# A fourth buffer for the projections' split weights, and other places for the pools of the up projection, in a decoder layer

## The chip, the cores and the metric

The kernel runs on one core of a Trainium2 chip. Its time is the device time of one execution in microseconds (us). The core has a matrix engine (PE in the profile), a vector engine (DVE), a scalar engine (ACT), GpSimd (POOL), and a sync engine (SP) from whose queue most DMAs are issued; each engine takes its instructions in the order in which they stand in its own list.

## What is computed

One layer of a hybrid decoder on a sequence of 1024 tokens of width 1024, in float32. Three branches (an mLSTM, a differential attention, a cross-attention into a memory) each give 1024 features per token; each is projected, weighted by a gate, and summed; one more projection and a residual follow, and then an MLP with a squared ReLU:

```python
merged = g_m * (y_m @ w_proj_m[l]) + g_d * (y_d @ w_proj_d[l]) + g_c * (y_c @ w_proj_c[l])
x = x + merged @ w_out[l]
h2 = rms_norm(x, norm_mlp_g[l])
x = x + jnp.square(jax.nn.relu(h2 @ w_up[l])) @ w_down[l]
```

The widths are 1024 to 1024 for the four projections, 1024 to 4096 for `w_up` and 4096 to 1024 for `w_down`. What stands ahead of these lines (norm, input projection, the three branches, the gates) isn't touched by the change.

## The kernel before

Features lie on the partitions and tokens along the free axis. Every float32 operand of a matmul is split into two parts of a shorter format, hi = cast(x) on ACT and lo = x - hi on DVE (`split`, lines L111 and L112, and `split2`, L104 and L67, whose DVE half keeps its place in the program's order). A product is then three matmuls (`mm3`, L91): hi with hi, weight hi with lo of the other operand, weight lo with hi. So PE's second matmul on an operand can't start before DVE has made its lo half.

The change lies in `tail()`, which has two stages and is followed by a third, `down()`.

**Projections.** The loop over the branches b = 2, 0, 1 loads the branch's output as eight tiles `kt` (`k_tiles`, L1382, raw tiles `kraw`), splits them into the nine places ys0 to ys8, and goes through four groups g of 256 output features. A group's weights come as two halves: `load_w` loads a raw tile of 128x1024 (L137, pool `rp2`, two buffers) and splits it into a `w` tile of twice the size (pool `wp2`, three buffers). A fourth pass over g does the output projection with `wout`: for each of the four quarters of a group, `res` adds the residual (L1475, tile `gl`), stores the new x (L1476, `x1_d`, in the profile x_d), squares it (L1481), adds the square to `ssq` on POOL (L1482), and stores x times the norm's gain (L1484, L1485, h2, in the profile h_d).

**Up projection.** `wino` runs a product of 2x2 blocks with seven products instead of eight (`PROD`), over 16 groups u of 256 output features, four steps kp each. A step needs the operand `xo` of kp (four of them, kept through the stage: loaded as `xr` from h2, combined into `xts` by `wino_t`, L1241 to L1244, and split) and a weight tile `wo`: a raw tile `wraw` (L1273, four places in turn, wr0 to wr3) on which POOL does four operations (`wino_s`, L1259 to L1262), split into one of four places in turn (wop1, wop20, wop21, wop22). 21 matmuls of 128x512 make a step; each of the seven sums has its own bank of PSUM. After a group DVE combines the banks into u2, c11, u3, c21 (pool `ev`), multiplies them by the norm's factor `rb` (L1516), ACT applies ReLU and Square into `rq` (L1517, L1518) and stores it to `r_d` (L1519); a generator resumed later makes `xts` of it and stores that too (L1522). The norm's factor is made in `rstd` from `ssq` in the midst of the first groups: 16 matmuls `px`, a copy `st` (L1532), a power on POOL.

**Down projection.** `down()` opens its own pools over the places of the up projection. Its operands `xd` are the rows of `r_d`, loaded by `xdma` (L1611) and split by `xsplit`; its weights `wo` have three places (dwo0 to dwo2) and its raw tiles three (dwr0 to dwr2). The operand of the first step, q = 0, is in three tiles: dx00 (products' operands 0 to 2), dx01 (3, 4) and dx02 (5, 6); those of q = 1, 2, 3 are in two tiles each. It goes in 16 passes of four steps, again 21 matmuls a step.

All pools of SBUF are stacked in the order in which they are opened, and a pool that is opened over the place of a closed one waits, tile by tile, until what lay there has been read for the last time. The order of the instructions on each engine is made by a scheduler when the program is built, except where PE's (`pinned`), DVE's (`self.V`) and the split's order are kept.

Of the kernel before, what the change touches and what calls it, by code (L numbers as in the profile page):

```python
# [10 lines left out]
F32 = mybir.dt.float32  # L11
# [6 lines left out]
P = 128  # L18
# [53 lines left out]
class Layer:  # L72
# [1338 lines left out]
    def tail(self):  # L1411
# [5 lines left out]
        def fetch(d, f, hf):  # L1417
            t = self.gl.tile([P, 512], F32, tag="gl", name=self.name("gl"))
            nc.sync.dma_start(t, half(d, f, hf))
            return t  # L1420

        c9 = ExitStack()
        with ExitStack() as c0:
            E = lambda *x, **k: c0.enter_context(tc.tile_pool(*x, **k))
# [8 lines left out]
            with ExitStack() as c1:  # L1433
                E = lambda *x, **k: c1.enter_context(tc.tile_pool(*x, **k))
                self.pmm, self.kmm, self.nmm = Banks(E, "pmm2"), 8, 3
                if True:

                    mtp = E(name="mtp", bufs=1)
                    mlp = E(name="mlp", bufs=16)
                    op = E(name="op", bufs=2)  # L1440
                    hole = E(name="hole", bufs=1).tile([P, 7 * 256], F32, name="hole")
                    V.memset(hole[:, 0:1], 0.0)
                    ysp = Ring([E(name=f"ys{i}", bufs=1) for i in range(9)][::-1])
                    rawp = E(name="yrp", bufs=2)
                    self.rp = E(name="rp2", bufs=2)
                    self.wp = E(name="wp2", bufs=3)
                    hi = [[mtp.tile([P, 512], F32R, name=f"mh{k}_{hf}") for hf in range(2)] for k in range(NK)]
                    mg, lo = {}, {}
                    for bi, b in enumerate((2, 0, 1)):
                        ys = self.k_tiles(ysp, rawp, self.yd[b])  # L1450
                        for g in range(4):

                            def merge(m, hf, ps):
                                ft = g * 2 + m
                                t = fetch(self.gdr, b * 8 + ft, hf)
                                if bi == 0:
                                    mg[ft, hf] = mlp.tile([P, 512], F32, tag="ml", name=self.name("mg"))
                                o = mg[ft, hf] if bi == 0 else t
                                V.scalar_tensor_tensor(out=o, in0=t, scalar=1.0, in1=ps, op0=ALU.add, op1=ALU.mult)
                                if bi == 1:  # L1460
                                    G.tensor_add(mg[ft, hf], mg[ft, hf], t)
                                if bi == 2:
                                    V.tensor_add(t, mg[ft, hf], t)
                                    lo[ft, hf] = mlp.tile([P, 512], F32R, tag="ml", name=self.name("ml"))
                                    self.split(hi[ft][hf], lo[ft, hf], t)

                            w = self.load_w(a[("wpm", "wpd", "wpc")[b]][g], 256, 4)
                            self.group(w, lambda k, i, hf: cut(ys[k], i, hf), merge, g == 0)
                    for g in range(4):

                        def res(m, hf, ps):
                            f = g * 2 + m
                            s = slice(hf * 512, (hf + 1) * 512)
                            x = fetch(a["xT"], f, hf)
                            V.scalar_tensor_tensor(out=x, in0=ps, scalar=0.5, in1=x, op0=ALU.mult, op1=ALU.add)  # L1475
                            nc.sync.dma_start(half(self.x1d, f, hf), x)  # L1476
                            if f == 0:
                                nc.scalar.activation(ssq[:, s], x, AF.Square)
                            else:
                                q = op.tile([P, 512], F32, tag="sq", name=self.name("sq"))  # L1480
                                nc.scalar.activation(q, x, AF.Square)  # L1481
                                G.tensor_add(ssq[:, s], ssq[:, s], q)  # L1482
                            h = op.tile([P, 512], F32, tag="h2", name=self.name("h2"))
                            nc.scalar.activation(h, x, AF.Copy, scale=self.vec[:, R_MLP + f : R_MLP + f + 1])  # L1484
                            nc.sync.dma_start(half(self.h2d, f, hf), h)  # L1485

                        w = self.load_w(a["wout"][g], 256, 4)
                        self.group(w, lambda k, i, hf: lo[k, hf] if i else hi[k][hf], res, g == 0)

            self.pw = Banks(lambda *x, **k: c9.enter_context(tc.tile_pool(*x, **k)), "pw")  # L1490
            with ExitStack() as c1:
                E = lambda *x, **k: c1.enter_context(tc.tile_pool(*x, **k))
                one_ = lambda n: E(name=n, bufs=1)
                xo2, xo3, wr2, wr3, self.ev, wop1, self.xtp, self.xrp, xo0, xo1, wr0, wr1 = (
                    one_(n)
                    for n in ("xo2", "xo3", "wr2", "wr3", "ev", "wop1", "xtp", "xrp", "xo0", "xo1", "wr0", "wr1")
                )
                wop2 = [one_(f"wop2{i}") for i in range(3)]
                self.xop = (xo0, xo1, xo2, xo3)
                self.wrp, self.wop = Ring([wr0, wr1, wr2, wr3]), Ring([wop1, *wop2])  # L1500
                dp, ap = one_("dgp"), one_("prt")

                def load(kp):
                    b = self.xrp.tile([P, 4, 512], F32, tag="xr", name=self.name("xr"))
                    nc.sync.dma_start(
                        b.rearrange("p (k h) n -> p k (h n)", k=2),
                        self.h2d[2 * kp : 2 * kp + 2].rearrange("k p n -> p k n"),
                    )
                    return b

                def use_up(u, cs):

                    b = self.xrp.tile([P, 4, 512], F32, tag="xr", name=self.name("rq"))
                    for i in (1, 3, 2, 0):
                        hf = i % 2
                        self.V.tensor_mul(cs[i], cs[i], rb[:, hf * 512 : (hf + 1) * 512])  # L1516
                        self.A.activation(cs[i], cs[i], AF.Relu)  # L1517
                        self.A.activation(b[:, i], cs[i], AF.Square)  # L1518
                    self.A.dma_start(self.rd[u, :, 0:3], b[:, 1:4])  # L1519
                    yield  # L1520
                    t = self.wino_t(b, self.V)
                    nc.sync.dma_start(self.rd[u, :, 3:7], t)  # L1522
                    yield

                def rstd():

                    bank = yield
                    ps = self.pw.tile([P, 512], F32, tag=bank, name=self.name("px"))
                    for t in range(NT):
                        self.mm(ps[:, t : t + 1], ssq[:, t * P : (t + 1) * P], ones[:, 0:1], start=True, stop=True)  # L1530
                    st = dp.tile([P, NT], F32, tag="st", name="st2")
                    V.tensor_copy(st, ps[:, 0:NT])  # L1532
                    self.rsqrt_mean(st, st, D, NT)
                    bank = yield
                    dg = dp.tile([P, NT, P], F32, tag="dg", name="dg")
                    for t in range(NT):
                        V.tensor_scalar_mul(dg[:, t], self.ident, st[:, t : t + 1])
                    for hf in range(2):
                        bank = yield
                        ps = self.pw.tile([P, 512], F32, tag=bank, name=self.name("px"))  # L1540
                        for i in range(4):
                            self.mm(ps[:, i * P : (i + 1) * P], ones, dg[:, hf * 4 + i], start=True, stop=True)
                        nc.scalar.copy(rb[:, hf * 512 : (hf + 1) * 512], ps)
                    yield

                rs = rstd()
                next(rs)

                def parts():
                    t = [ap.tile([P, 512], F32, name=f"pt{i}") for i in range(3)]  # L1550
                    t += [self.gl.tile([P, 512], F32, tag="gl", name=f"pt{i}") for i in (3, 4)]
                    q = sp.tile([P, D], F32, tag="ssq", name="pt5")
                    return t + [q[:, 0:512], q[:, 512:]]

                self.wino([a["wup"][u] for u in range(16)], load, use_up, rs.send, parts)
# [340 lines left out]
```

## Time and profile before

| | |
|---|---|
| median of 3 runs | 2207.19 us (2204.16 to 2207.41) |
| the profiled execution | 2206.06 us, span of its records 2204.3 us |
| mean granted clock of PE | 0.994 of full speed |
| PE busy | 2156.7 us, 98% of the span |
| DVE, ACT, POOL busy | 1422.7, 1001.4, 566.6 us |
| moved by DMA | 281.46 MB, 128 GB/s on the mean |

The profile of one execution is read by views. The chain of waits follows the work back from the last instruction. The view of waits lists by engine and line what an engine sat idle for. The view of groups gives count, busy time and mean duration (ns) of instructions of one line, operation and shape. The view of windows gives, for each stretch, the busy time of each engine with the number of its instructions, and at the end PE's granted clock (1.00 is full speed), the share of DMA engines busy and the GB/s moved. The timeline lists instructions by start and length, merged where they are alike, with the idle time before them in brackets. The projections' part that the change touches begins at about 1190 us, the up projection at 1566 us, the down projection at 1885 us.

### The profile page before, as it was taken

To read this page: it belongs to the slowest core of one execution; us is meant where nothing else is said; L and a number is where in the kernel's file an instruction comes from. 1 tells how busy PE (TensorE), PEld (TensorE's weight loads), DVE (VectorE), ACT (ScalarE), POOL (GpSimd) and SP (SyncE) were. 2 spreads that over 40 slices of the span, in tenths; PEclk is the share of its full clock that TensorE was granted. 3 is DMA by queue.
4 is the path that set the end of the run, shared out by engine and by line. 5 is a ranking of instruction groups with operands and counts; after the bars stand their busy time and mean duration, and the time that the engine had idled before them with its cause. 6 is when DMAs were issued, how large, how long until landed. Compare 5 with 4: busy or idle time off the path is not lost.

```text
span 2204.3 us, 30709 instructions
## 1 busy us (share of the span) xinstructions
PE 2156.7 (98%) x11049; PEld 1856.0 (84%) x11049; DVE 1422.7 (65%) x2678; ACT 1001.4 (45%) x1998; POOL 566.6 (26%) x732
## 2 busy tenths in 40 slices
PE   7999999999999999999999999999999999999999
PEld 5877888898799999999878888887787888788887
DVE  6643565575447877777665432544688877867779
ACT  6543354454246666666554220224444444543332
POOL 2100000000211111111031003202657655565553
PEclk9999999999999999999999999999999999999999
DMA  6113222121443333333254543436435444854444
GB/s 244 36 68 116 62 91 68 44 82 48 150 126 92 89 88 93 94 82 82 84 170 131 204 149 119 139 110 210 151 111 197 158 149 147 322 195 156 143 142 166
DMA packets 137358, 281.46 MB, mean 128 GB/s; under 512 B 13137, under 2 KB 29814, under 8 KB 135158
## 3 DMA queue, kind: packets, MB, share of 16 engines
q1 hardware_dynamic: 130870, 259.58, 37.5%
q10 hardware_dynamic: 6336, 19.93, 2.3%
q8 instruction: 87, 1.43, 0.3%
q14 instruction: 65, 0.53, 0.1%
HBM read 182.95 MB, written 71.34 MB: 115 GB/s over the span
## 4 chain that ended last, share of the span: by engine, by line
PE 80%; DVE 7%; DMA 7%; ACT 2%; POOL 2%; issue 2%; SPq 0%; DVEq 0%; ACTq 0%; POOLq 0%
PE mm L91 47%; PE p L91 20%; PE sc L91 6%; PE po L91 3%; PE tp L94 3%; DVE acc L67 1%; DVE wo L67 1%; DMA wraw<-in_wdown 1%; PE pr L94 1%; DMA xd<-r_d 1%; DMA xr<-h_d 1%; DVE w L112 1%; DMA gl<-in_xT 1%; DMA x_d<-gl 1%; DMA raw<-in_wd 0%
## 5 line engine op out<-in xcount | busy, mean ns | idle before, releaser
L91 PE MATMUL mm<-w,hT 128*128 128x384 f32 (+3 forms) x2496 | 475.5, 333 | 6.9 <-ACT w L111 5.9
L91 PE MATMUL mm<-hT,w 128*128 128x512 f32 x1680 | 411.8, 396 | 0.0
L91 PEld LDWEIGHTS mm<-w,hT 128*128 128x128 f32 x2496 | 391.8, 190 | 19.3 <-ACT w L111 7.2
L91 PEld LDWEIGHTS mm<-hT,w 128*128 128x128 f32 x1680 | 308.5, 188 | 64.7
L91 PE MATMUL p<-xo,wo 128*128 128x512 f32 x1344 | 309.9, 392 | 6.3 <-DVE st L1532 3.2
L91 PE MATMUL p<-xd,wo 128*128 128x512 f32 x1344 | 310.0, 393 | 4.4 <-DVE c L67 1.8
L91 PEld LDWEIGHTS p<-xo,wo 128*128 128x128 f32 x1344 | 252.2, 189 | 62.7 <-DVE u L67 3.7
L91 PEld LDWEIGHTS p<-xd,wo 128*128 128x128 f32 x1344 | 254.0, 190 | 60.2 <-DVE c L67 2.9
L91 PE MATMUL mm<-kt,w 128*128 128x512 f32 x1152 | 262.3, 389 | 0.8 <-DVE kt L112 0.8
L91 PEld LDWEIGHTS mm<-kt,w 128*128 128x128 f32 x1152 | 215.9, 188 | 47.1 <-DVE kt L112 1.4
L111 ACT CAST w<-raw 128x256 fp32r<-128x256 f32 (+3 forms) x272 | 142.3, 545 | 155.5 <-PE mm L91 124.5
L112 DVE TENSOR_TENSOR w<-raw,w 128x256 fp32r<-128x256 f32 (+3 forms) x272 | 161.1, 613 | 76.7 <-ACT w L111 76.0
L104 ACT CAST wo<-wraw 128x896 fp32r<-128x896 f32 x122 | 114.9, 944 | 206.8 <-PE p L91 109.7
L67 DVE TENSOR_TENSOR wo<-wraw,wo 128x896 fp32r<-128x896 f32 x122 | 144.5, 1201 | 60.1 <-ACT wo L104 60.0
L1259 POOL TENSOR_TENSOR wraw<-wraw 128x128 f32<-128x128 f32 x128 | 95.9, 749 | 245.2 <-DMA wraw<-in_wdown 106.8
L1007 ACT ACTIVATE dpe<-sc,dst,drr 128x256 f32<-128x256 f32 (+7 forms) x128 | 106.6, 833 | 96.6 <-DVE dst L1003 91.8
L127 POOL TENSOR_SCALAR hss<-hss 128x4 f32<-128x4 f32 x8 | 3.3, 409 | 415.2 <-ACT mscr L752 272.9
L999 DVE CUSTOM_DVE_ANT_0 sc<-sc,tmask 128x256 f32<-128x256 f32 (+7 forms) x128 | 97.2, 759 | 14.0 <-PE sc L91 13.4
L91 PE MATMUL sc<-dk,dq 128*128 128x512 f32 (+3 forms) x384 | 92.2, 348 | 0.0
L1262 POOL TENSOR_TENSOR wraw<-wraw 128x128 f32<-128x128 f32 x128 | 88.2, 689 | 9.9
L1261 POOL TENSOR_TENSOR wraw<-wraw 128x128 f32<-128x128 f32 x128 | 88.7, 693 | 0.0
L104 ACT CAST xd<-xd 128x1536 fp32r<-128x1536 f32 (+2 forms) x36 | 54.9, 1528 | 72.0 <-DMA xd<-r_d 72.0
(308 smaller groups left out, 3093.3 us busy)
## 6 DMA issues: line engine op xcount, KB each, us to landing
dk<-dsg SPq DMA_DIRECT2D x64, 256.0 KB, 4.3
wraw<-in_wup SPq DMA_DIRECT2D x64, 256.0 KB, 3.3
r_d<-xts SPq DMA_DIRECT2D x16, 1024.0 KB, 4.1
wraw<-in_wdown SPq DMA_DIRECT2D x64, 256.0 KB, 3.1
xd<-r_d SPq DMA_DIRECT2D x19, 768.0 KB, 7.6
xd<-r_d SPq DMA_DIRECT2D x14, 1024.0 KB, 7.2
raw<-in_wd SPq DMA_DIRECT2D x32, 384.0 KB, 3.3
kraw<-y SPq DMA_DIRECT2D x24, 512.0 KB, 4.2
```

The source lines that it names most:

```text
L67: return self.tc.keep_in_program_order(f(*a, **k))
L91: self.pin(self.nc.tensor.matmul(out, l, r, start=start, stop=stop))
L94: self.pin(self.nc.tensor.transpose(out, x, self.ident))
L104: self.A.copy(hi, src)
L111: nc.scalar.copy(hi, src)
L112: nc.vector.tensor_sub(lo, src, f32(hi))
L127: g.tensor_scalar(r, ss, 1.0 / width, EPS, op0=ALU.mult, op1=ALU.add)
L999: V.tensor_tensor_reduce(out=sc[:, 0:n], in0=sc[:, 0:n], in1=self.tmask[:, D - n : D], scale=1.0, scalar=-3.0e38, op0=ALU.add, op1=ALU.max ...
L1007: nc.scalar.activation(pe[c][:, 0:n], sc[:, 0:n], AF.Exp, bias=t8[:, 2 + c : 3 + c], scale=rr[:, i, c : c + 1], accum_out=t8[:, 4 + c : 5 ...
L1259: G.tensor_add(r[:, 4], r[:, 0], r[:, 3])
L1261: G.tensor_sub(r[:, 6], r[:, 1], r[:, 0])
L1262: G.tensor_sub(r[:, 7], r[:, 2], r[:, 5])
```

## The change

The diff has two edits in `tail()`; `down()` isn't edited.

```diff
-                    hole = E(name="hole", bufs=1).tile([P, 7 * 256], F32, name="hole")
+                    hole = E(name="hole", bufs=1).tile([P, 2824], F32, name="hole")
...
-                    self.wp = E(name="wp2", bufs=3)
+                    self.wp = E(name="wp2", bufs=4)
...
-                xo2, xo3, wr2, wr3, self.ev, wop1, self.xtp, self.xrp, xo0, xo1, wr0, wr1 = (
+                xo2, xo3, wr3, self.ev, dp, wr2, wop1, self.xtp, self.xrp, xo0, xo1, wr0, wr1 = (
                     one_(n)
-                    for n in ("xo2", "xo3", "wr2", "wr3", "ev", "wop1", "xtp", "xrp", "xo0", "xo1", "wr0", "wr1")
+                    for n in ("xo2", "xo3", "wr3", "ev", "dgp", "wr2", "wop1", "xtp", "xrp", "xo0", "xo1", "wr0", "wr1")
                 )
...
-                dp, ap = one_("dgp"), one_("prt")
+                ap = one_("prt")
```

The first edit gives the projections' split weights a fourth buffer and makes the unused tile `hole` 4128 bytes longer per partition (11296 instead of 7168), so that all that is opened after it lies 4128 bytes higher. The second opens the pool `dgp` of `rstd` (4128 bytes) and the place wr2 of the third raw tile inside the stack, ahead of wop1, instead of dgp near its end and wr2 ahead of wr3. wr2, and not a place that a merged tile held, now lies over the hole. In the built programs the pools stand at these bytes of each partition:

| pool | before | after |
|---|---|---|
| hole | 89600 to 96768 | 89600 to 100896 |
| wp2 | 186880 to 211456 | 191008 to 223776 |
| wr2, third raw tile | 73216 to 77312 | 89632 to 93728 |
| wr3 | 77312 to 81408 | 73216 to 77312 |
| ev (u2, c11, u3, c21) | 81408 to 89600 | 77312 to 85504 |
| dgp | 200192 to 204320 | 85504 to 89632 |
| wop1, xtp, xrp, xo0, xo1, wr0, wr1, wop20 to wop22 | 89600 to 200192 | the same order from 93728 to 204320 |
| xo2, xo3; prt | 15872 to 73216; 204320 to 210464 | unchanged |

The pools of `down()` keep their places, so they lie over others of the up projection. dx00 (200192 to 212480) lay over dgp and prt, and lies over wop22 and prt. dx02 (73216 to 81408) lay over wr2 and wr3, and lies over wr3 and half of ev. dwr0 and dwr1 lay over wr0 and wr1, and lie over the end of xo1 and over wr0. dx1 lay over xo0, and lies over the end of xrp and xo0. dx2 lay over xo1, and lies over xo0 and xo1.

The scheduler puts the instructions in another order at the places that wait for these. The number behind a name tells tiles of one name apart.

DVE before, in the output projection's first two groups; w_2453 and w_2455 are the halves of the third group's weights, w_2473 and w_2475 those of the fourth, the lines L1475 the residual adds of the quarters that PE finishes one by one:

```order
L1475 SCALAR_TENSOR_TENSOR gl_2424_14923<-mm_2419_14816,gl_2424_14923 128x512
L112 TENSOR_TENSOR w_2453_15103<-raw_2452_15101,w_2453_15103 128x1024
L1475 SCALAR_TENSOR_TENSOR gl_2426_14931<-mm_2420_14817,gl_2426_14931 128x512
...
L1475 SCALAR_TENSOR_TENSOR gl_2449_15091<-mm_2448_15066,gl_2449_15091 128x512
L112 TENSOR_TENSOR w_2455_15108<-raw_2454_15106,w_2455_15108 128x1024
L112 TENSOR_TENSOR w_2473_15253<-raw_2472_15251,w_2473_15253 128x1024
```

The same place after:

```order
L112 TENSOR_TENSOR w_2453_15103<-raw_2452_15101,w_2453_15103 128x1024
...
L1475 SCALAR_TENSOR_TENSOR gl_2424_14923<-mm_2419_14816,gl_2424_14923 128x512
L112 TENSOR_TENSOR w_2455_15108<-raw_2454_15106,w_2455_15108 128x1024
L1475 SCALAR_TENSOR_TENSOR gl_2426_14931<-mm_2420_14817,gl_2426_14931 128x512
...
L1475 SCALAR_TENSOR_TENSOR gl_2449_15091<-mm_2448_15066,gl_2449_15091 128x512
L112 TENSOR_TENSOR w_2473_15253<-raw_2472_15251,w_2473_15253 128x1024
L112 TENSOR_TENSOR w_2475_15258<-raw_2474_15256,w_2475_15258 128x1024
```

Each half stands one buffer earlier: w_2455 ahead of the residual adds from gl_2426 to gl_2449, six of them, instead of behind them.

ACT before, at the end of the up projection; rq_2844 is the last group's squared output, xd_2850, xd_2854 and xd_2855 are operands of the down projection's first two steps:

```order
L111 CAST wo_2853_18270<-wraw_2851_18252 128x7x128
L111 CAST xd_2850_18250<-xd_2850_18250 128x2x512
L111 CAST xd_2854_18273<-xd_2854_18273 128x3x512
L111 CAST xd_2855_18275<-xd_2855_18275 128x4x512
L1313 COPY u2_2840_18116<-p0_2831_18016 128x512
L111 CAST wo_2856_18277<-wraw_2852_18258 128x7x128
L111 CAST wo_2860_18294<-wraw_2857_18280 128x7x128
```

ACT after, from the second weight tile of the down projection on; xd_2848 is the tile in dx00, which the down projection's first matmul reads:

```order
L111 CAST wo_2860_18294<-wraw_2857_18280 128x7x128
L111 CAST xd_2859_18292<-xd_2859_18292 128x4x512
...
L1518 ACTIVATE rq_2844_18128<-u3_2842_18118 128x512
L1518 ACTIVATE rq_2844_18128<-u2_2840_18116 128x512
L1519 DMA r_d<-rq_2844_18128 128x1536
L111 CAST xd_2848_18246<-xd_2848_18246 128x3x512
L104 CAST xd_2862_18307<-xd_2862_18307 128x3x512
L111 CAST xd_2850_18250<-xd_2850_18250 128x2x512
L104 CAST xd_2863_18309<-xd_2863_18309 128x4x512
L111 CAST xd_2854_18273<-xd_2854_18273 128x3x512
L104 CAST wo_2875_18374<-wraw_2861_18297 128x7x128
L111 CAST xd_2855_18275<-xd_2855_18275 128x4x512
```

In the list before, the cast of xd_2848 stands 164 rows ahead of the cast of wo_2853, about 100 us into the up projection; now it stands behind all of rq_2844, and so do xd_2850, xd_2854 and xd_2855. On DVE the low halves of these tiles stand behind the three L67 operations of xts_2845, the last group's.

SP after, the same place; a DMA from r_d into an xd tile is issued when its place is free:

```order
L1273 DMA wraw_2852_18258<-in_wdown 128x512
L1611 DMA xd_2858_18290<-r_d 128x3x512
L1611 DMA xd_2859_18292<-r_d 128x4x512
L1611 DMA xd_2848_18246<-r_d 128x3x512
L1273 DMA wraw_2861_18297<-in_wdown 128x512
L1611 DMA xd_2862_18307<-r_d 128x3x512
L1611 DMA xd_2863_18309<-r_d 128x4x512
L1611 DMA xd_2850_18250<-r_d 128x2x512
L1273 DMA wraw_2871_18339<-in_wdown 128x512
L1522 DMA r_d<-xts_2845_18142 128x2048
L1611 DMA xd_2854_18273<-r_d 128x3x512
L1611 DMA xd_2855_18275<-r_d 128x4x512
```

The load of xd_2848 waits for the last matmul of the up projection (the reader of the tile in wop22), that of xd_2850 for the last Square that reads u2, those of xd_2854 and xd_2855 for the landing of the store of rq_2844. In the list before, the load of xd_2848 waited for the store of the first group's rq. Two further moves are in the lists: the load of the third raw tile, wraw_2499, moves from the up projection's first steps to the first projection's start (row 439 of SP's list to row 298), with its four POOL operations, and at that start the splits of the first two `kt` tiles stand ahead of the first half of the weights instead of around it.

## The prediction

> **What bounds the kernel now.** I read the page first, for the whole.
>
> ```profile
> span 2204.3 us, 30709 instructions
> ...
> PE 2156.7 (98%) x11049; PEld 1856.0 (84%) x11049; DVE 1422.7 (65%) x2678; ACT 1001.4 (45%) x1998; POOL 566.6 (26%) x732
> ```
>
> PE is busy 98% of the time. The matmuls stay as they are, so the change can only move what PE waits for and the clock that it gets. Next comes the view of PE's waits from the projections' start (1190 us) to the end.
>
> ```profile
> PE p L91 <- DVE st L1532: 3.2, 1, 3.2
> PE p L91 <- DVE u L67: 2.9, 4, 1.3
> PE mm L91 <- DVE w L112: 2.7, 1, 2.7
> PE p L91 <- DVE c L67: 2.5, 3, 1.1
> ...
> PE mm L91 <- DVE kt L112: 0.8, 1, 0.8
> PE p L91 <- POOL wraw L1260: 0.8, 1, 0.8
> ```
>
> Three of these are what the change is near: `kt` 0.8 at the first projection, `w` 2.7 in the output projection, `st` 3.2 at the up projection's start. That is 6.7 us in all. The others are mostly at the start of the down projection, which the timeline of PE shows (start, length, count, idle time before).
>
> ```profile
> 1854.73 30.76 PE L91 MATMUL p<-xo,wo 128*128 128x512 f32 x135
> 1885.33 1.52 PE L91 MATMUL p<-xd,wo 128*128 128x512 f32 x6
> 1887.95 0.96 PE L91 MATMUL p<-xd,wo 128*128 128x512 f32 x3 [1.10 <-DVE c L67]
> 1889.67 1.56 PE L91 MATMUL p<-xd,wo 128*128 128x512 f32 x3 [0.75 <-POOL wraw L1260]
> 1892.57 1.65 PE L91 MATMUL p<-xd,wo 128*128 128x512 f32 x3 [1.33 <-DVE u L67]
> 1894.91 11.28 PE L91 MATMUL p<-xd,wo 128*128 128x512 f32 x38 [0.70 <-DVE c L67]
> ```
>
> The up projection runs at 30.76/135 = 0.228 us a matmul up to T = 1885.33, where the down projection begins. Then the windows, for the clock (the third number from the end).
>
> ```profile
> 1582.00:1584.00 2.00, 2.00 (x7) 1.53 (x6) 1.83 (x2) 2.00 (x6) 2.00 (x2) 0.63 0.41 127
> 1584.00:1586.00 2.00, 2.00 (x6) 1.60 (x5) 2.00 (x4) 2.00 (x3) 2.00 (x4) 0.51 0.50 131
> ...
> 1890.00:1895.00 5.00, 2.96 (x7) 1.34 (x6) 4.14 (x5) 5.00 (x4) 3.52 (x4) 0.50 1.05 403
> 1895.00:1900.00 5.00, 5.00 (x12) 3.74 (x13) 5.00 (x6) 1.57 (x3) 2.71 (x4) 0.50 0.29 83
> ...
> 1905.00:1925.00 20.00, 20.00 (x90) 16.41 (x89) 16.95 (x16) 10.66 (x13) 15.16 (x17) 1.00 0.91 319
> ```
>
> A wait costs more than itself: behind the `st` wait the clock is low for 4 us, a loss of 2 x 0.37 + 2 x 0.49 = 1.7 us, and at the down projection it is halved from 1890 to 1900, with 12 matmuls in 5 us. So the first two steps of the down projection, 42 matmuls, which would take 9.6 us at 0.228, end only at the 27th of the last row's 38: 12 of them by 1900, 15 more in 3.4 us, at 1903.4 = T + 18.1.
>
> **The gains.** The first is `kt`: the two first kt splits stand ahead of the weights' half on DVE, which earlier held one of them up; the wait of 0.8 goes, or stays if the loads of kraw come late. The second is `w`: w_2455 is split six residual adds sooner, so PE's 2.7 us there go. What is late next is the sum `ssq`, which the 16 matmuls px need.
>
> ```profile
> 1566.44 6.28 PE L91 MATMUL p<-xo,wo 128*128 128x512 f32 x27
> 1572.56 1.84 PE L91 MATMUL px<-ones,ssq 128*128 128x1 f32 x16
> 1574.26 3.71 PE L91 MATMUL p<-xo,wo 128*128 128x512 f32 x15
> 1581.18 11.18 PE L91 MATMUL p<-xo,wo 128*128 128x512 f32 x41 [3.22 <-DVE st L1532]
> ```
>
> The last add of ssq on POOL:
>
> ```profile
> 1570.50 2.02 POOL L1482 TENSOR_TENSOR ssq<-ssq,sq 128x512 f32<-128x512 f32 x1 [3.43 <-ACT sq L1481]
> ```
>
> It ended at 1572.52, and px began at 1572.56, without slack. If that add doesn't come sooner, PE gives the 2.7 us back as a wait ahead of px. Then only the third gain counts: wraw_2499's four POOL operations no longer stand between the add and the raw tile that DVE's queue needs before `st`, some 2.5 of the 3.2 us (the 3.6 us of four such operations in POOL's rows below, less the low half of a weight tile, 1.1, that still stands ahead of `st`); with kt that makes 3.3. If the add does come sooner (the 512 KB load of w_2475's raw tile and a weight tile's load no longer share the DMA engines with the stores that the chain goes through), all 6.7 go, and with them the clock's 1.7: 8.4. I take the middle between 3.3 and 8.4, about 5, since it hangs on loads whose overlap I can't time; both ends stay in the range, with 2.5 as the lower one, without kt.
>
> **The cost.** In the trace of before, the operand of the down projection's first matmul (xd_2848, in dx00) was loaded and split in the midst of the up projection. The view of tile xd from 1655 to 1680 us ends with
>
> ```profile
> L111 ACT CAST xd<-xd x2: 1049/1266/1483, 1662.6 to 1670.4; 128x1536 fp32r<-128x1536 f32 x1, 128x1024 fp32r<-128x1024 f32 x1
> ...
> DMA to landing us min/median/max: 4.6/4.6/4.6
> ```
>
> that is, over 200 us ahead of its use. With the change dx00 lies over wop22, whose last reader is the up projection's last matmul: the load can't be issued before T, and its cast stands on ACT behind the whole output of the last group, its low half on DVE behind xts_2845. The other operands of the first two steps are late in the same way. The durations, from the groups between 1850 and 1905 us (mean ns at the end of the middle field):
>
> ```profile
> L67 DVE TENSOR_TENSOR xts<-rq,xts 128x512 f32<-128x512 f32 x4 | 4.9, 1214 | 0.1
> L112 DVE TENSOR_TENSOR xd<-xd 128x2048 fp32r<-128x2048 f32 x2 | 4.6, 2288 | 0.2 <-ACT xd L111 0.2
> L67 DVE TENSOR_TENSOR u<-u,rb 128x512 f32<-128x512 f32 x6 | 4.1, 728 | 0.0
> L112 DVE TENSOR_TENSOR xd<-xd 128x1536 fp32r<-128x1536 f32 x2 | 3.6, 1795 | 0.2 <-ACT xd L111 0.2
> L1517 ACT ACTIVATE u<-u 128x512 f32<-128x512 f32 x6 | 3.5, 616 | 0.0
> L112 DVE TENSOR_TENSOR wo<-wraw,wo 128x896 fp32r<-128x896 f32 x3 | 3.3, 1111 | 1.3 <-ACT wo L111 1.3
> L111 ACT CAST xd<-xd 128x1536 fp32r<-128x1536 f32 x2 | 2.9, 1473 | 0.0
> L111 ACT CAST wo<-wraw 128x896 fp32r<-128x896 f32 x3 | 2.8, 946 | 5.1 <-POOL wraw L1262 3.6 <-PE p L91 1.6
> L67 DVE TENSOR_TENSOR xts<-rq 128x512 f32<-128x512 f32 x2 | 1.4, 692 | 3.2 <-ACT rq L1518 3.2
> ```
>
> The least that the order allows, with ACT and DVE free at T: wo_2860, over wop22 too, cast to T + 0.9 and low half to 2.1; the last add of u2 (0.7, as long as a multiply) to 2.8; four multiplies, the first at 3.5, the fourth at 5.7. ACT then does four ReLUs and four Squares, 8 x 0.616 = 4.9, to 8.4, and the cast of xd_2848 to **9.9: PE's first matmul**. DVE goes on from 5.7 with xd_2858 and xd_2859 (1.80, 2.29) to 9.8, xts (0.69 + 2 x 1.21) to 12.9 and xd_2848 (1.80) to **14.7: the second matmul**. The load of xd_2848, 4.6 to 9.3 us (rows here), is hidden under this.
>
> It can be later. dwr0 and dwr1 now lie over xo1, so the down projection's first two raw tiles are loaded only from T - 9.6 (42 matmuls before T). Loads in these 55 us, and one tile's POOL work, by its first and last row:
>
> ```profile
> r_d<-rq ACTq DMA_DIRECT2D x3, 768.0 KB, 6.3
> wraw<-in_wdown SPq DMA_DIRECT2D x7, 256.0 KB, 5.2
> xd<-r_d SPq DMA_DIRECT2D x4, 768.0 KB, 9.3
> ```
>
> ```profile
> 1886.22 1.39 POOL L1259 TENSOR_TENSOR wraw<-wraw 128x128 f32<-128x128 f32 x1 [9.87 <-DMA wraw<-in_wdown]
> ...
> 1889.36 0.45 POOL L1262 TENSOR_TENSOR wraw<-wraw 128x128 f32<-128x128 f32 x1
> ```
>
> Landing at T - 4.4, twice 3.6 us of POOL to T + 2.8, then wo_2856's cast and low half to 4.9; behind these on DVE stand three adds (2.2), wo_2860, the last add and the multiplies: about 4.7 us later than in the least case. So the second matmul is between T + 14.7 and T + 19.4; I take 17, since the least case needs both engines idle at T and the other a full load time and slow POOL.
>
> The rest of the first step is 20 matmuls, after a pause of 10 us and more at the halved clock as from 1895 to 1900: 12 in 5.0 us, 8 in 1.8. It ends at 21.5 to 26.2. The second step needs xd_2854, whose load waits for the landing of rq_2844's store: issued at 8.4 to 13.1, landed 6.3 later, then a load of 4.6 to 9.3, cast and low half (3.3): 22.6 to 32.0. Behind that stand on DVE wo_2875, xd_2863 and xd_2855 (1.1 + 2.3 + 2.3), so PE's eighth matmul of the step, the second to use xd_2855, runs at 28.3 to 37.7, and the last 14 take 3.2: T + 31.5 to T + 40.9, with one more clock loss of 1.7 at the upper end. Against T + 18.1 that is 13.4 to 24.5 us later; from the middles (17 for the second matmul, 10.7 for the store, 7 for the load) it is T + 36, or **18 us**. Steps three and four use xd_2858 to xd_2863, split by then, and the passes behind them keep their order of work, so I cost them at nothing: DVE was busy for 16.95 of the 20 us from 1905 to 1925, and if its queue falls behind there, some us are added. Nothing gives the time back, PE being 98% busy.
>
> The clock's share in this: the rows show it halved after four waits of at most 1.33 us each, and full only after 5 us without a wait. The Trainium skill ("TensorE: Matmul & The Clock Gate", Part 1) says that the half rate comes after an idle window of about 3.4 us and ends after a busy one of about 3.4 us. By that the restart would cost 8 slow matmuls instead of 12, 0.8 us less, and the old waits should not have halved the clock; this trace disagrees on the second.
>
> **Sum.** 2206.06 (the profiled execution) - 5 + 18 = 2219. The median of the runs is 1.1 us above the profiled one, so I put the forecast at 2220.
>
> **Rivals.**
> *The cost at its least and the gain whole*, 13.4 - 8.4 = +5, 2212; with a us less on either side it would be within 0.2% (4.4 us, about what a measurement of this kernel can tell from no change). For it: the least case skips no instruction. Against: it needs every load at its shortest, and the DMA engines ran at 403 GB/s and a share of 1 here.
> *The cost at its most, without the gain* (the add of ssq doesn't move, kt neither): 24.5 - 2.5 = +22, 2229. For it: px had no slack. Against: POOL's work there does go.
> *Faster*: the down projection's start isn't gated by dx00's place. The one point that decides is when the load of xd_2848 is issued. If it were released by an earlier reader, say the one that ends three steps before T (14.4 us), load, cast and low half would fit into ACT's and DVE's idle time ahead of the last group's output, the old start at T + 18.1 would stay, and the gain alone would count: 2207 - 5 = 2202. For it: only 4128 of the 7168 bytes of wop22's tile are shared with dx00. Against: the release is of the whole tile, its last products are read by the last matmul, and the order on ACT and DVE is fixed behind the last group anyhow.
>
> **How the numbers follow.** My forecast, between +9 and +17, 0.62; the cost near its least with the gain whole 0.17 (a quarter of it within 0.2%); the cost near its most 0.15; the faster case 0.04, and 0.02 for a start that cancels by chance. That makes slower 0.90, within 0.2% 0.06, faster 0.04. The range is from 2211 (+4, the least cost and the whole gain) to 2228 (+21), which leaves out little more than the faster case and the very top.
>
> **What would show it.** Right: a wait of PE of 9 us or more at the first matmul of p<-xd, put down to ACT xd L111 or DVE xd L112, a second one in the next step, a halved clock over some 5 us behind each, the first load of xd issued at the end of p<-xo; the waits at w (2.7) gone and at st smaller. Wrong: a first p<-xd less than 8 us behind the last p<-xo, or a wait of over 3 us ahead of px that eats the gain and more, or new waits after the first pass of the down projection.

## The result: slower by 0.67%, and the profile after

The changed kernel takes 2223.93 us (median of 6 runs, 2220.01 to 2224.65) against 2208.66 us of the kernel before beside it (6 runs, 2204.16 to 2211.41): a ratio of 1.0067, 95% interval 1.0056 to 1.0078, some 15 us. The profiled execution took 2224.29 us, with a span of 2222.5 us.

PE's waits from 1190 us on, in the changed kernel:

```profile
PE p L91 <- ACT xd L111: 13.4, 3, 11.9
PE p L91 <- DVE xd L112: 8.5, 3, 4.7
PE px L91 <- POOL ssq L1482: 1.7, 1, 1.7
PE p L91 <- DVE u L67: 1.6, 3, 0.8
PE mm L91 <- DVE kt L112: 1.1, 2, 0.7
PE p L91 <- DVE st L1532: 0.6, 1, 0.6
```

The wait at `w` (2.7 us) is gone and that at `st` has shrunk from 3.2 to 0.6; that at `kt` is 1.1 instead of 0.8, and 1.7 us for `ssq` are new. Two new lines head the list, both for `xd`, the operands of the down projection: 21.9 us in six waits. The old waits there, for c, u and wraw, are gone. The timeline of PE shows where they lie:

```profile
1877.66 7.16 PE L91 MATMUL p<-xo,wo 128*128 128x512 f32 x30
1896.72 0.76 PE L91 MATMUL p<-xd,wo 128*128 128x512 f32 x1 [11.89 <-ACT xd L111]
1902.18 6.46 PE L91 MATMUL p<-xd,wo 128*128 128x512 f32 x20 [4.70 <-DVE xd L112]
1909.10 0.51 PE L91 MATMUL p<-xd,wo 128*128 128x512 f32 x1 [0.47 <-ACT xd L111]
1910.90 1.43 PE L91 MATMUL p<-xd,wo 128*128 128x512 f32 x5 [1.29 <-DVE xd L112]
1913.34 0.49 PE L91 MATMUL p<-xd,wo 128*128 128x512 f32 x1 [1.02 <-ACT xd L111]
1916.30 28.93 PE L91 MATMUL p<-xd,wo 128*128 128x512 f32 x120 [2.46 <-DVE xd L112]
```

Each pair is one operand: a single matmul as soon as ACT has cast it, the rest when DVE has made its low half. ACT's timeline shows the cast of xd_2848 right behind the last Square and its store, as the order has it:

```profile
1894.12 1.13 ACT L1518 ACTIVATE rq<-u 128x512 f32<-128x512 f32 x2
1894.77 0.33 ACTq L1519 DMA_DIRECT2D r_d<-rq  x1
1895.17 1.46 ACT L111 CAST xd<-xd 128x1536 fp32r<-128x1536 f32 x1
```

Eleven more kernels are called e1 to e11 and explained below. Cut into stages by the starts of the first and the last matmul of each kind, the profiled executions of those that bear on this stand as follows (us; no edit touches the stage ahead of the first column, and the projections start between 1209 and 1213.5):

| kernel | projections | up projection's matmuls | its end to the down projection's last matmul |
|---|---|---|---|
| before | 352.9 | 318.7 | 314.2 |
| the change | 352.5 | 320.3 | 333.1 |
| e2, down pools moved | 351.9 | 322.4 | 315.0 |
| e3, and 64-byte places | 351.3 | 320.8 | 315.1 |
| e5, and all 5120 higher | 349.0 | 321.5 | 311.7 |
| e11, the change 5120 higher | 348.8 | 319.5 | 332.1 |
| e4, 32 bytes ahead of wp2 | 361.3 | 316.0 | 313.7 |
| e9, fourth buffer alone | 351.3 | 323.3 | 313.5 |
| e8, the change, dx00 moved | 351.1 | 319.9 | 332.8 |
| e10, the change, all but dx02 moved | 351.4 | 324.1 | 331.1 |

The cost is 18.9 us at the start of the down projection. The gain ahead of it, which I had put at 5, is +0.4 - 1.6 = -1.2 by this table. Each row is a single execution: e8 and e10 have the change's first two stages as they are and took 671.0 and 675.5 us for them, against 672.8 in the change and 671.6 before, so this number is good to some 2 us. A gain of 5 isn't there, and that was the surprise. The windows of 30 us show half of its cause. In the kernel before, a window in the output projection and one in the up projection:

```profile
1530.00:1560.00 30.00, 30.00 (x134) 24.86 (x133) 12.80 (x11) 10.66 (x13) 10.81 (x10) 1.00 0.62 208
1800.00:1830.00 30.00, 30.00 (x134) 24.84 (x133) 23.31 (x29) 11.79 (x17) 18.95 (x30) 1.00 0.44 159
```

The same windows of the changed kernel, with one in the first projections ahead of them:

```profile
1260.00:1290.00 30.00, 30.00 (x134) 24.82 (x134) 6.16 (x8) 2.11 (x2) 0.00 (x0) 1.00 0.32 103
1530.00:1560.00 30.00, 30.00 (x130) 24.15 (x129) 11.11 (x11) 9.40 (x12) 14.03 (x10) 1.00 0.64 200
1800.00:1830.00 30.00, 30.00 (x131) 24.40 (x131) 22.73 (x29) 10.94 (x16) 17.02 (x27) 1.00 0.43 149
```

PE is busy without a gap and at full clock (1.00), and yet does 130 or 131 matmuls instead of 134. Three matmuls take 0.700 us from start to start instead of 0.680, all through the output projection, and in the up projection in two of the four steps of a group, those that read xo2 and xo3. In the first projections the pace is the old one.

### The profile page after: what moved, and what is told of

Its sections match the earlier page's. It is cut to its first block, busy times and chain, and to the rows that moved or that the text cites. A ratio compares the mean times of both kernels' runs of the same rounds, so it can differ in the third digit from the quotient of the medians.

```text
span 2222.5 us, 30719 instructions
## 1 busy us (share of the span) xinstructions
PE 2160.8 (97%) x11049; PEld 1854.4 (83%) x11049; DVE 1422.3 (64%) x2678; ACT 1002.2 (45%) x1998; POOL 564.6 (25%) x732
## 4 chain that ended last, share of the span: by engine, by line
PE 83%; DMA 6%; DVE 6%; ACT 2%; issue 2%; POOL 1%; SPq 0%; DVEq 0%; ACTq 0%; POOLq 0%
PE mm L91 47%; PE p L91 23%; PE sc L91 6%; PE po L91 3%; PE tp L94 3%; DMA xr<-h_d 1%; DVE acc L67 1%; DMA xd<-r_d 1%; PE pr L94 1%; DMA kraw<-y 1%; DVE u L67 1%; DMA h_d<-h 0%; DMA raw<-in_wd 0%; DVE w L112 0%; DMA x_d<-gl 0%
## 5 line engine op out<-in xcount | busy, mean ns | idle before, releaser
L91 PE MATMUL p<-xo,wo 128*128 128x512 f32 x1344 | 313.7, 395 | 2.2 <-DVE u L67 1.6
L67 DVE TENSOR_TENSOR wo<-wraw,wo 128x896 fp32r<-128x896 f32 x122 | 143.1, 1190 | 69.4 <-ACT wo L104 69.4
```

The lines of the kernel that those rows point to most:

```text
L67: return self.tc.keep_in_program_order(f(*a, **k))
L91: self.pin(self.nc.tensor.matmul(out, l, r, start=start, stop=stop))
```

## The experiments

The theory at this point: the loss is the start of the down projection, since its pools lie over places that the up projection frees last (P), and the gain was eaten by the slower pace, which comes from the new addresses (A). The rivals: the loss has another cause than those places; the pace is chance.

**e1: places at multiples of 64 bytes.** The change puts what lies behind the hole 4128 bytes higher, 32 past a multiple of 64.

```diff
-hole = E(name="hole", bufs=1).tile([P, 2824], F32, name="hole")
+hole = E(name="hole", bufs=1).tile([P, 2832], F32, name="hole")
...
-st = dp.tile([P, NT], F32, tag="st", name="st2")
+st = dp.tile([P, 2 * NT], F32, tag="st", name="st2")[:, 0:NT]
```

> The change with 32 bytes more in hole and 32 bytes more in dgp, so that every tile that the change had put at 32 past a multiple of 64 bytes stands at a multiple of 64 again; the order of all instructions is that of the change. Theory: where PE's two operands stand at different remainders of 64 bytes, three matmuls take 0.700 us instead of 0.680 (output projection, and the half of the up projection that reads xo2 and xo3); that ate 384 x 0.0067 + 672 x 0.0067 = 7 us of the gain. Then this runs at 0.680 throughout and takes about 2217 us, 7 less than the change, with the stall at the down projection's start as it was. Rival: the slower pace is chance of the profiled run; then the time is the change's, 2224, and some runs show the slow pace whatever the places.

Measured: 2223.89 us, ratio to before 1.0078 (1.0055 to 1.0101). The pace stayed slow in the same places. So 64 bytes aren't the step; whether the pace is chance was still open.

**e2: the down projection's pools over their old partners.** On the change:

```diff
-x02 = one_("dx02")
 a2 = one_("acc2")
-accum(a2, 4, 0)
+accum(a2, 4, 1024)
+x02, _ = one_("dx02"), one_("dpad").tile([P, 8], F32, name="dpad")
```

> The change, with the pools of the down projection moved so that they lie over the same pools of the up projection as before (dx02 over dgp and wr2, dx00 over prt, all others 4128 bytes higher). Theory: the loss is the stall at the down projection's start, so 17 to 18 us go; the down projection's tiles now stand in part at 32 past a multiple of 64, which by the theory of the pace costs 528 x 0.0067 = 3.5 us there: about 2210 us. If the pace doesn't depend on places: about 2206. If the loss has another cause than the places of the down projection's tiles: 2224.

Measured: 2205.72 us against 2205.2, ratio 1.0002 (0.9990 to 1.0015). The edit changes no operation, only places and the order where these are waited for. The last column of the table is back at 315.0, and nothing of the loss that can be told is left: P holds. What the change does ahead of the down projection comes to nothing that can be told. The 2210 that were expected with a slow pace in the down projection weren't reached, though the pace was slow there: 520 of its matmuls lie 32 bytes off and took 3.4 us more by their starts. In this execution the clock stayed at 1.00 from 1885 to 1905, where the kernel before had 0.50 for 10 us; half of the 8 us that PE was busy in these, an estimate of 4 us, goes the other way.

**e3: both.** e1 and e2 together, with the pad at 16 floats.

> Both edits of the two runs before together: the down projection's pools over their old partners, and all tiles at multiples of 64 bytes. Theory of places and pace: 2224 - 17.5 - 7 = 2199, some 9 us faster than before, which is the change's own gain (6.7 us of waits and 1.7 us of low clock). If the pace doesn't depend on places: as the run with the pools moved alone.

Measured: 2204.58 us, ratio 0.9997 (0.9985 to 1.0008). No gain over e2, in line with e1.

**e4: 32 bytes ahead of wp2, in the kernel before.** A test of the addresses alone: nothing else moves and the order of all instructions is that of before.

```diff
-self.wp = E(name="wp2", bufs=3)
+self.wp = [E(name="wpad", bufs=1).tile([P, 8], F32, name="wpad"), E(name="wp2", bufs=3)][1]
```

> The kernel before with 32 bytes ahead of the pool wp2 and nothing else; the order of all instructions is that of before. Only the split weights of the projections stand at 32 past a multiple of 64, their other operands at 0. Theory: all 1536 matmuls of the four projections take 0.0067 us more, so 10 us slower than before, 2219, with 0.700 us for three matmuls from 1210 to 1566. Rival: no effect, 2208.7.

Measured: 2213.52 us against 2205.2, ratio 1.0030 (1.0016 to 1.0045): slower by 6.6 us by the ratio, 8.3 by the medians. The timeline of PE over the same 30 us, first of before, then of e4:

```profile
1339.62 30.76 PE L91 MATMUL mm<-kt,w 128*128 128x512 f32 x135
```

```profile
1339.73 30.50 PE L91 MATMUL mm<-kt,w 128*128 128x512 f32 x130
```

Less the last matmul's own 0.39 us, that is 30.37/134 = 0.2266 and 30.11/129 = 0.2334 us a matmul. So the pace is no chance: it hangs on the distance between the two operands' places. The projections take 8.4 us longer, not 10, as the wait at w shrinks from 2.7 to 1.6 us beside it. With e1 (both operands 4160 higher in the first projections: fast; only the weights higher in the output projection: slow) it is the distance that counts and not the place.

**e5: the distance kept to 1024.** e3 with everything 5120 bytes higher instead of 4160: `[P, 3072]` in hole, 256 floats of st, 256 of the pad.

> The kernel with both edits (down projection's pools over their old partners), but all tiles behind the hole 5120 bytes higher than before instead of 4160, so that every address keeps its remainder of 1024; the order of all instructions is that of the run with both edits. Theory: the pace of the matmuls hangs on the distance of the two operands by some step of more than 64 and at most 1024 bytes; the slow pace (130 to 132 matmuls in 30 us instead of 134) goes in the output, up and down projections, 11 us in all: about 2194, faster than before by 11. Rival: the pace hangs on something else; then it is the 2204.6 of the run with both edits.

Measured: 2198.76 us against 2208.16, ratio 0.9964 (0.9953 to 0.9975): faster than before by 8 us, and than the changed kernel by more. The windows have 134 matmuls in 30 us everywhere again:

```profile
1530.00:1560.00 30.00, 30.00 (x134) 24.86 (x133) 12.07 (x11) 9.20 (x12) 15.75 (x11) 1.00 0.64 203
1800.00:1830.00 30.00, 30.00 (x134) 24.85 (x133) 23.70 (x31) 11.50 (x17) 17.21 (x27) 1.00 0.43 150
```

Of the 11 us expected over e3, 7 came by the two ratios. By the table 2.3 came in the projections and 3.4 in the down projection, and nothing in the up projection, where PE now comes earlier to the matmuls px and waits for the sum, and waits once more 80 us later, for a copy of a bank of PSUM:

```profile
1568.05 1.02 PE L91 MATMUL px<-ones,ssq 128*128 128x1 f32 x8 [0.73 <-DVE gl L1475]
1570.75 1.74 PE L91 MATMUL px<-ones,ssq 128*128 128x1 f32 x8 [1.68 <-POOL ssq L1482]
...
1649.70 4.06 PE L91 MATMUL p<-xo,wo 128*128 128x512 f32 x15 [1.99 <-ACT u L1313]
```

**e8 and e10: which place costs.** The theory of the prediction had three late chains, for dx00, dx02 and dx1. e8 moves dx00 alone, e10 all of them but dx02:

```diff
-x00 = one_("dx00")
+x00 = [one_("dpad").tile([P, 1032], F32, name="dpad"), one_("dx00")][1]
```

```diff
-x1, x2 = one_("dx1"), one_("dx2")
+x1, x2 = [one_("dpad").tile([P, 1032], F32, name="dpad"), one_("dx1"), one_("dx2")][1:]
```

> The change with only dx00 moved, 4128 bytes up, over prt and free space, so that the operand of the first matmul is loaded and split early again. The theory of the prediction took each late tile as a wait of its own, with the second step's operand (dx1) the one that ends last: then the first matmuls run early, PE waits for xd_2850 in the first step and for xd_2854 and xd_2855 in the second as in the change, and the time is within 1 us of the change's 2224. If the first operand is what costs, some 10 us go: 2214.

> The change with dx1, dx2, dwr0, dwr1, dwo0 to dwo2 and dx00 moved 4128 bytes up over their old partners, and dx02 left over ev. Theory: PE waits in the first step alone, for xd_2850, whose load follows the last Square of u2; the first step's last 12 matmuls run from T + 16 or 17 at the halved clock and end at T + 22, the second step at T + 27 instead of T + 36: 2215, 9 less than the change. If dx02 costs nothing by itself: 2206.

Measured: e8 2225.03 us, ratio 1.0086 (1.0069 to 1.0103), as expected; e10 2223.34 us, ratio 1.0076 (1.0061 to 1.0091), where I had expected 2215. PE in e8, then in e10:

```profile
1882.44 2.25 PE L91 MATMUL p<-xd,wo 128*128 128x512 f32 x9
1899.35 0.76 PE L91 MATMUL p<-xd,wo 128*128 128x512 f32 x1 [14.65 <-DMA acc<-x_d]
1901.19 4.76 PE L91 MATMUL p<-xd,wo 128*128 128x512 f32 x11 [1.07 <-DVE xd L112]
1908.40 0.50 PE L91 MATMUL p<-xd,wo 128*128 128x512 f32 x1 [2.45 <-ACT xd L111]
1912.02 23.31 PE L91 MATMUL p<-xd,wo 128*128 128x512 f32 x94 [3.12 <-DVE xd L112]
```

```profile
1886.41 2.24 PE L91 MATMUL p<-xd,wo 128*128 128x512 f32 x9
1907.20 0.76 PE L91 MATMUL p<-xd,wo 128*128 128x512 f32 x1 [18.54 <-ACT xd L111]
1908.41 26.89 PE L91 MATMUL p<-xd,wo 128*128 128x512 f32 x105 [0.45 <-DVE xd L112]
```

In both, the first nine matmuls run at once and PE then stops for xd_2850 in dx02. (The "DMA acc" in e8's bracket names one of several waits; ACT's cast of xd_2850 ended at 1899.26.) In e10 that stop alone is 18.5 us, for a reason that SP's timeline shows,

```profile
1901.23 0.37 SPq L1611 DMA_DIRECT2D xd<-r_d  x1
```

and ACT's:

```profile
1894.29 1.90 ACT L104 CAST xd<-xd 128x2048 fp32r<-128x2048 f32 x1 [1.01 <-DMA xd<-r_d]
1896.59 0.63 ACT L1517 ACTIVATE c<-c 128x512 f32<-128x512 f32 x1 [0.40 <-DVE c L67]
...
1906.05 1.05 ACT L111 CAST xd<-xd 128x1024 fp32r<-128x1024 f32 x1 [4.84 <-DMA xd<-r_d]
```

The load of xd_2850 can only be issued when the last Square has read u2 of the pool ev, at 1901.2, 15 us after the end of the up projection, and not the 10 I had taken: with the other operands early, DVE and ACT put their splits ahead of the last group's multiplies and Squares. It landed at 1906. The second step of e10 ended 32.0 us after the up projection, 4.4 us sooner than in the change and 5 later than I had expected. Another 3.4 us of the miss aren't in the expectation at all: with the pools moved by 4128 bytes, 518 matmuls of the down projection run at the slow pace, which the change doesn't have there. So dx02 alone is enough for most of the loss, and freeing dx00 alone buys nothing. A kernel in which dx00 alone or dx1 alone is late was not run.

**e9: the fourth buffer alone**, in the kernel before (`bufs=4`, nothing else).

> The kernel before with the fourth buffer of wp2 alone; hole, wr2, dgp and all places of before stay. Theory: PE's wait of 2.7 us at w and of 0.8 at kt go, the matmuls keep the pace of before, and the down projection its start; the add of ssq and then st decide how much is given back: 2202 to 2206, 0 to 3 us less than before. Rival: the fourth buffer gives nothing, since the residual chain ends last: 2205.

Measured: 2205.85 us, ratio 0.9992 (0.9978 to 1.0005): no difference that can be told. The waits from 1190 to 1600 us:

```profile
PE px L91 <- DVE gl L1475: 2.0, 1, 2.0
PE p L91 <- DVE st L1532: 1.8, 1, 1.8
PE px L91 <- POOL ssq L1482: 1.4, 1, 1.4
```

The 2.7 us at w are gone and 3.4 us ahead of px have come. The chain that ends last here is that of the residual: its last add on DVE waits for the load of its x tile (pool `gl`, two buffers), and square and sum follow.

```profile
1569.78 0.69 DVE L1475 SCALAR_TENSOR_TENSOR gl<-mm,gl 128x512 f32<-128x512 f32 x1 [4.69 <-DMA gl<-in_xT]
```

DVE waits as long there in the changed kernel (4.73 us) and 4.09 us in the kernel before.

**e6 and e7: the pace by distance.** The kernel before with four places for w that are used in turn, each at another distance past a multiple of 1024 bytes from the other operand (e7 has pads of 16, 80 and 160 floats):

```diff
-self.wp = E(name="wp2", bufs=3)
+self.wp = Ring([E(name="wp20", bufs=1), [E(name="wpad1", bufs=1).tile([P, 32], F32, name="wpad1"), E(name="wp21", bufs=1)][1], ...])
```

> The kernel before with four places for the split weights of the projections, at 0, 128, 256 and 512 bytes past a multiple of 1024 from the other operand's, used in turn; everything else stays in place. A measurement of the pace by distance: each half of a group's weights serves 48 matmuls, so the trace shows stretches of about 11 us at each of the four distances. Theory: 0.680 us for three matmuls at the distances that are multiples of the step, 0.700 at the others; if the step is 128 all four are at 0.680, if it is 512 those at 128 and 256 are at 0.700, if it is 1024 only the first is at 0.680. Rival (the pace hangs on which tiles are live or on the order, not on the distance): all four stretches alike.

> As the run with 0, 128, 256 and 512, with distances of 0, 64, 384 and 1024 bytes. Theory: 0.680 us for three matmuls at 0 and 1024, 0.700 at 64; 384 tells 128 from 256 as the step. Rival: all alike.

Measured, in one execution each: 2206.63 and 2213.72 us, beside 2205.63 of before. The timeline of PE in e6 over three stretches, with the weights at 0, at 128, and at 256 and 512 in turn:

```profile
1300.92 10.81 PE L91 MATMUL mm<-kt,w 128*128 128x512 f32 x47
...
1311.80 11.54 PE L91 MATMUL mm<-kt,w 128*128 128x512 f32 x49
...
1323.65 20.56 PE L91 MATMUL mm<-kt,w 128*128 128x512 f32 x90
```

and in e7 at 0, at 64, and at 384 and 1024 in turn:

```profile
1303.69 10.59 PE L91 MATMUL mm<-kt,w 128*128 128x512 f32 x46
...
1314.80 10.40 PE L91 MATMUL mm<-kt,w 128*128 128x512 f32 x44
...
1326.67 20.52 PE L91 MATMUL mm<-kt,w 128*128 128x512 f32 x88
```

By (length - 0.39)/(count - 1): 0.2265, 0.2323, 0.2266 and 0.2267, 0.2328, 0.2314 us. Fast at 0, 256 and 512, slow at 64 and 128, between the two where 384 and 1024 alternate. Told apart by the addresses in the built program, the matmuls at 384 took 0.232 us from start to start on the median and those at 1024 0.227. The step that fits all is 256 bytes.

**e11: the change, 5120 bytes higher.** The hole and the `st` of e5 on the change, with the down projection's pools as in the change.

> The change with its tiles 5120 bytes higher than before instead of 4128, so that all keep their remainder of 256 against those that didn't move; the order of all instructions and the pools of the down projection are the change's, so the stall at the down projection's start stays. Theory: the slow pace in the output projection and in half of the up projection goes, 7 us (384 + 672 matmuls by 0.0067): 2217 against the change's 2224. Rival: the slow pace was paid for elsewhere, or the stall grows by what comes sooner: 2224.

Measured: 2217.18 us against 2206.79, ratio 1.0048 (1.0032 to 1.0064). So the pace alone accounts for some 4 (by the ratios, whose intervals overlap) to 7 us (by the medians) of the change's 15. The stall at the down projection's start is still there: 17.9 us by the table. PE's waits from 1190 to 1600 us show why not all of the pace comes back:

```profile
PE px L91 <- DVE gl L1475: 2.5, 1, 2.5
PE px L91 <- POOL ssq L1482: 1.7, 1, 1.7
```

They have 4.2 us ahead of px, where the change has 1.7.

## Why the prediction was right, and where it was off

*The cost.* Right in kind and size: 18 us forecast, 18.9 measured. Against the end of the up projection (T = 1884.67, where the next matmul would have started) the first matmul came at T + 12.0 (9.9 in the least case), the second at T + 17.5 (17), the first with xd_2854's low half at T + 26.2 (27.3 by the middles), the eighth of the second step at T + 31.6 (33), and the step's end at T + 36.4 (36). It was worked out from the order on ACT and DVE and from durations of the trace. The sums of single instructions held to 1.4 us over 35; that the end agrees to half a us is luck in part, as the last 14 matmuls came sooner and then took 4.7 us at a low clock instead of 3.2. One sum of the working is wrong: by its own terms the late case puts the second matmul 6.1 us behind the least case and not 4.7 (to 4.9, then adds of 2.2 and wo_2860's low half of 1.1, against 2.1), so the top of its range would be 1.4 us later; the forecast of 17 doesn't hang on it.

*The parts of it.* Right that xd_2848 is not the part that ends last (e8). Not seen: that the late xd_2850 costs most of it by itself (e10), as early operands go ahead of the last group's output on the same engines.

*The clock.* The pause halved it, as forecast. It was full again 3.6 us after PE went on at 1902.18, behind 8 slow matmuls, and not behind the 12 in 5 us that the forecast took from the kernel before; 8 was the count that it set beside them. The second, shorter row of waits cost 0.34 x 5 = 1.7 us once more, which the forecast had for its upper end. Windows of the changed kernel:

```profile
1902.00:1904.00 2.00, 1.82 (x4) 1.49 (x5) 2.00 (x3) 0.92 (x1) 2.00 (x2) 0.50 1.10 324
1904.00:1906.00 2.00, 2.00 (x7) 1.52 (x6) 1.45 (x2) 0.00 (x0) 1.92 (x3) 0.57 0.84 262
1906.00:1908.00 2.00, 2.00 (x10) 1.67 (x9) 0.00 (x0) 0.42 (x1) 0.31 (x1) 1.00 1.06 409
...
1910.00:1915.00 5.00, 1.93 (x6) 1.05 (x6) 5.00 (x4) 3.49 (x3) 0.00 (x0) 1.00 0.99 365
1915.00:1920.00 5.00, 3.70 (x10) 2.96 (x11) 1.25 (x1) 1.88 (x2) 3.12 (x8) 0.66 1.05 402
```

Between 1910 and 1915 PE was busy 1.93 of 5 us and kept its full clock; the fall came behind it.

*The gain.* This is the step that failed: "I take the middle between 3.3 and 8.4, about 5". By the stages it was -1.2, and e2, which is the change without its stall, stands at +0.5 us against before (-2.2 to +3.3), with a slower pace and a better clock behind it. Three things are wrong in it. The middle of its two ends is 5.9, not 5. The add of ssq didn't come sooner: it ended 361.4 us after the first matmul on `kt`, against 359.0 in the kernel before, and PE waits 1.7 us ahead of px for it, in e9 3.4. So the lower case, 3.3, was the right one, though partly by luck: 2.7 came at w and 2.6 at st, 1.7 went ahead of px, and at kt nothing came (0.3 more). And the term of the pace was missing: "The matmuls stay as they are, so the change can only move what PE waits for and the clock that it gets." They stay in number and order, but not in place, and 0.0067 us more on 384 matmuls of the output projection and on half of the up projection's 1344 are 7 us in full, of which e11 gave back 4 to 7. With 3.3 and 7 in the place of 5 the sum would have been 2206 - 3.3 + 7 + 18 = 2228, more than 3 above the profiled execution. A part of that is that what PE loses in pace it waits less for ssq (1.7 us ahead of px against 4.2 in e11), so the two terms don't simply add up; another is that the changed kernel's projections began 1.9 us sooner than in before.

*The size.* The forecast of +13 and the measured +15 lie close since the errors are small beside the cost. That the loss comes from the places of the down projection's pools is shown by e2, and that dx02's is enough for most of it by e10; that the gain is lost to pace and to the chain of ssq is shown by e5, e9 and e11. In e5 the up projection takes 2.8 us more than in before, with the pace of before. By the starts of the matmuls 0.9 of this lies in the first 20 us, where waits ahead of px stand in the place of the one at st, and 2.0 between 80 and 120 us, where PE waits the 1.99 us for ACT's copy that are shown with e5; before waits 0.42 there. Why that copy comes late in e5 stays open.

## What to carry to other kernels

A pool that is moved moves everything that lies over it later. Before a buffer is added, list for each later pool which old pool it overlaps and when that one is read for the last time, through to stages that the diff doesn't touch; an operand that was loaded hundreds of us ahead can turn into one that waits for the last matmul of the stage before. Then compare addresses, not only orders: if two operands of the same matmuls change their distance, keep its remainder, here of 256 bytes. And where a wait of PE sits ahead of a chain that ends last anyway, taking it away only moves it.

## What was not expected of the hardware

The pace of back-to-back matmuls of 128x512 float32r hung on the distance of the places of weights and moving operand: 0.2266 us each where it was a multiple of 256 bytes away from that of before (0, 256, 512, 1024, 5120), 0.232 to 0.233 us where it was off by 32, 64, 128, 384, 4128 or 4160, with PE's records at full clock and without a gap. Sorted by the addresses in the built programs, the matmuls of all thirteen profiled kernels from the first projection on, without those behind a wait or at a low clock, take 0.2269 us on the mean where the distance is a multiple of 256, and 0.2333, 0.2333, 0.2324 and 0.234 us where it is 32, 64, 128 and (in e8 alone) 224 past one. 2.5 to 3% of a matmul's time hangs on it. Why is not shown by any run here.

The clock didn't answer alike to like waits. At the start of the down projection the kernel before and e3 wait for the same engines, for 3.9 and 4.3 us in four waits each; before had a clock of 0.50 from 1890 to 1900, e3 had 1.00 from 1880 to 1900:

```profile
1885.00:1890.00 5.00, 2.68 (x9) 1.46 (x9) 4.90 (x6) 4.13 (x4) 3.07 (x6) 1.00 1.03 397
1890.00:1895.00 5.00, 4.25 (x18) 3.49 (x19) 5.00 (x7) 3.80 (x4) 2.87 (x5) 1.00 0.56 178
```

So some us between two profiled executions at such a place can be the clock's and not the kernel's work. What decides it no run here shows.
